# Making a product's operands one step later, and one low part by an accumulating DMA

## The chip, the cores and the metric

The kernel runs on one core of one Trainium2 chip. Its time is the device time of one execution in microseconds (us), given as the median of several runs; lower is better. The core has a matrix engine (TensorE, PE in the profile), a vector engine (VectorE, DVE), a scalar engine (ScalarE, ACT), GpSimd (POOL) and SyncE (SP), each with an instruction queue of its own that is worked through in order, and 16 DMA engines that SP, ACT and POOL can give transfers to. Engines wait for each other by semaphores.

## The reference

Two layers of a decoder trunk on 512 tokens of width 1024, in float32. What bears on the change is the feed-forward block (swiglu), of which there are two in each layer, so four in all:

```python
D_MODEL = 1024
SEQ = 512
DEPTH = 2
D_FF = 2816

def rms_norm(x, gain):
    xf = x.astype(jnp.float32)
    inv = lax.rsqrt(jnp.mean(xf * xf, axis=-1, keepdims=True) + NORM_EPS)
    return (xf * inv).astype(x.dtype) * gain

def swiglu(h, w_gate, w_up, w_down):
    return (jax.nn.silu(h @ w_gate) * (h @ w_up)) @ w_down

def reference(x, ...):
    for l in range(DEPTH):
        x = x + 0.5 * swiglu(rms_norm(x, ffn1_norm[l]), ffn1_wg[l], ffn1_wu[l], ffn1_wd[l])
        h = rms_norm(x, mix_norm[l])
        z = h @ w_in[l]
        ...
        x = x + jnp.concatenate([attn_out, conv_out], axis=-1) @ w_out[l]
        x = x + 0.5 * swiglu(rms_norm(x, ffn2_norm[l]), ffn2_wg[l], ffn2_wu[l], ffn2_wd[l])
    return rms_norm(x, final_norm)
```

## The kernel before

**Every float32 matrix is split in two.** TensorE multiplies fp32r tiles, a rounded form of float32. Each operand is made into a high part (a rounding cast on ScalarE) and a low part (the value less the high part, a subtraction on VectorE), by `split` (line 204); a product is then three matmuls: high by high, high by low, low by high. For the weights these parts are called `wh` and `wl` (pools of three buffers each), and line 205 and line 206 of the profile are the cast and the subtraction of every split in the kernel.

**Products of 2 x 2 blocks are made with seven multiplications instead of eight.** The class `Seven` (line 662) makes the seven operands of one side from four blocks b11, b12, b21, b22 of activations: b11, b21 and b22 as they are, and four sums t1 to t4 (lines 681 to 687: t1 = b11 - b12, which overwrites b12; t2 and t3 from b12 - b22; t4 = t2's value + b21). Each is then split into a pair of tiles named `fb...` or `ft...`, from a pool of eight. `make` makes an operand when it is first asked for. The seven operands of the other side are made from weights as `need_split` (line 215) goes along: its forms are a11, a12, s2, s3, s1, a22, s4 in the order of the seven products, two half tiles (h = 0, 1) each. The tiles are loaded by SP into a pool of eight raw buffers; the second summand of a weight sum is added by POOL in an accumulating DMA (line 200); s2 is made by an addition in place on VectorE (`tensor_add(a11, a11, s1)`, line 233) ahead of its split, and s4's input by another accumulating DMA (line 261).

**The shares.** In each feed-forward block two groups of 512 of the 2816 rows of `w_down` are worked off by `share` (line 895), so there are eight shares in the kernel: s_0_2 and s_0_6 in the first block, s_1_1 and s_1_5, s_2_1 and s_2_5, s_3_1 and s_3_5 in the others. A share goes through seven steps, one product each, written by `stream` (line 878) as 2 x 12 matmuls at line 884:

```python
CHAINS = (
    ("x", "b11", True), ("w", "b21", True), ("x", "t2", False), ("y", "t3", True),
    ("x", "t1", False), ("y", "t4", False), ("x", "b22", False),
)
```

The second name is the activations' operand and the first the accumulator (x_s, w_s, y_s in the profile). Step 2 is thus the product of t2 with the weights' sum s2. The first block's second share has its own order (`CHAINS_EARLY`: b11, b21, t3, t2, t4, t1, b22, the last into an accumulator of its own, z_s). After a step's last matmul VectorE adds the accumulator into the stream x (line 923).

Before the change, once step 0, 1 or 2 has been written, `share` asks for the operand of the step four on: after step 0 that of step 4, after step 1 that of step 5, after step 2 that of step 6. The operands of steps 0 to 3 have been made by then, during the stage ahead (`ahead`). The mixing stage calls `share` too, with a list of its own (`soon`), and makes its operands t1 and b22 by `split_far` (line 209), in which the low part is made without VectorE:

```python
    def split_far(hi, lo, raw):
        nc.scalar.activation(lo, raw, AF.Copy, scale=-1.0)
        state["cast"] = nc.scalar.copy(hi, raw)
        return nc.gpsimd.dma_start(out=f32(lo), in_=raw, accum_op=ALU.add)
```

ScalarE writes the negated rounded value into `lo` (line 211) and the rounded value into `hi` (line 212), and POOL issues a DMA (line 213) that adds the value itself into `lo`.

**The order of work.** Instructions are written in program order and a scheduler arranges each engine's queue from its own estimates and the buffers' dependences; some regions are arranged by hand (`by_hand`, from step 4 of the first block's second share on). So a call that is moved in the source moves instructions in the queues, and others close up around them.

Of the kernel before, what the change touches and what calls it, by code (L numbers as in the profile page):

```python
# [73 lines left out]
def trunk_kernel(  # L74
# [32 lines left out]
    def psum(tag, shape, name):  # L107
        return ps.tile(shape, F32, tag=tag, bufs={"mm": 4, "sc": 2, "aux": 2}[tag], name=name)
# [4 lines left out]
    def g8(name, dt=F32R, shape=(P, 2, 2, S)):  # L113
        return work.tile(list(shape), dt, tag="g8", bufs=4, name=name)
# [165 lines left out]
    def take_split(ahead=SPLIT_AHEAD):  # L280
        n = state["group"]
        state["group"] += 1
        need_split(n + ahead)
        return n, *split_of.pop(n)
# [20 lines left out]
    def by_hand():  # L305
        state["region"] = tc.manual_schedule(engines={pe})
        state["region"].__enter__()
# [180 lines left out]
    def xt(t, o):  # L488
        return stream_of[2 * o + t // 2][:, t % 2, :]
# [388 lines left out]
    def stream(accs, wh, wl, xh, xl, h, start, norm=None):  # L878

        for u in range(2):  # L880
            tok = slice(u * P, (u + 1) * P)
            for k in range(2):
                for i, (x_, w) in enumerate(((xh, wh), (xl, wh), (xh, wl))):
                    nc.tensor.matmul(  # L884
                        accs[u],
                        x_[:, 2 * h + k, tok],
                        w[:, k, :],
                        start=start and h + k + i == 0,
                        stop=h + k == 2 and i == 2,
                        skip_group_check=not start,  # L890
                    )
            if norm:
                norm.pull()

    def share(
        ops, by, between=None, soon=None, after=None, each=lambda: None, w=None, kept=()
    ):


        accs = {}  # L900
        chains, shares = (CHAINS_EARLY, SHARES_EARLY) if after else (CHAINS, SHARES)
        for step, (acc, operand, start) in enumerate(chains):
            ops.make(operand)
            if after and step == 4:
                by_hand()
            xh, xl = ops.forms[operand]
            if acc == "w" and w:
                accs[acc], start = w, False
            if start:
                tag = {"x": "mm", "y": "sc", "w": "aux", "z": "mm"}[acc]  # L910
                accs[acc] = [psum(tag, [P, S], f"{acc}_{ops.name}_{m}") for m in range(2)]
            for h in range(2):
                _, wh, wl = take_split()
                stream(accs[acc], wh, wl, xh, xl, h, start, after if step == 6 else None)
                each()
                if soon:
                    ops.make(*soon.get((step, h), ()))
                if h == 0 or step in kept:
                    continue
                for o, t, sign in shares[step]:  # L920
                    for m in range(2):
                        part = xt(2 * t + m, o)
                        nc.vector.scalar_tensor_tensor(  # L923
                            part, accs[acc][m], by * sign, part, op0=ALU.mult, op1=ALU.add
                        )
                        if after and (step, (o, t)) in ENDS_EARLY:
                            after(2 * t + m, o)
            if not soon and step < 3:
                ops.make(chains[step + 4][1])
            if between:  # L930
                between(step)
        return accs
# [5 lines left out]
    def ahead(ops, at):  # L938
        return lambda step: ops.make(*at.get(step, ()))


    def ffn(norm, stages, whole, after=None, late=None):
# [228 lines left out]
                pending.setdefault(clock[0] + tick, []).append(lambda do=do, n=n: do(n))  # L1171

        def shared(b):
            return Seven([raw_act(b), raw_act(b + 2)], room_form, f"s_{whole}_{b}")

        def raw_act(b):
            if b not in raws:
                raws[b] = g8(f"raw_a_{whole}_{b}", F32, (P, KC // 2, S))
            return raws[b]
# [13 lines left out]
        for i, (what, b) in enumerate(stages):  # L1193
# [3 lines left out]
            if what in "wu" and stages[i + 1][0] == "s":  # L1197
                ops = shared(sevens[0])
                if what == "w":
                    winograd2(b, i, ahead(ops, {3: ("b11",), 4: ("b21",), 5: ("t2",), 6: ("t3",)}))  # L1200
                else:
                    winograd(b, ahead(ops, {1: ("b11",), 2: ("b21",), 4: ("t2",), 6: ("t3",)}))
            elif what == "w":
                winograd2(b, i)
            if what == "s" and b == sevens[0]:
                then = shared(sevens[1])
                sums = ("t3", "t2") if stages[-1] == ("s", sevens[1]) else ("t2", "t3")
                soon = ahead(then, {3: ("b11",), 4: ("b21",), 5: sums[:1], 6: sums[1:]})
                goes_on = stages[i + 1][0] == "d"
                accs = share(ops, 0.5, soon, each=turns, kept=(1, 5, 6) if goes_on else (1,))  # L1210
                w = accs["w"]
                open_ = going_on(accs) if goes_on else {}
            elif what == "s":
                accs = share(
                    then,
                    0.5,
                    each=turns,
                    after=after if final else None,
                    w=w,
                    kept=() if final else (1, 5, 6),  # L1220
                )
                open_ = going_on(accs) if not final else {}
# [153 lines left out]
    def mix(l, norm, after):  # L1376
# [184 lines left out]
        ops.make("b21", "b22")  # L1561
        after.begin()
        share(ops, 1.0, soon={(0, 1): ("t3",), (1, 0): ("t2",), (1, 1): ("t1", "t4")}, after=after)
        state["late"] = None

# [42 lines left out]
```

## Time and profile before

| what | value |
|---|---|
| median of 3 runs | 1658.65 us (1658.05 to 1659.65) |
| the profiled execution, its own time | 1658.03 us |
| its span, first to last instruction | 1656.3 us |
| matmuls on PE | 7912 |
| mean granted TensorE clock | 0.999 |
| DMA moved | 299.77 MB, mean 181 GB/s |

The profile is one execution of the program, seen by the hardware's profiler. A row of a timeline gives the start from the span's beginning, the duration, the engine, the line of the kernel, the operation, the tiles written and read with buffer numbers left out, their shape, and how many such instructions follow each other; in brackets stands how long the engine had been idle before and what ended that. A row of waits gives who waited for whom, the total in us, how often, and the longest. A row of windows gives a stretch, its length, each engine's busy time with its number of instructions, then the granted clock, the share of the 16 DMA engines' time and GB/s. A row of DMA issues gives size and the median time from issue to landing. Matmuls are pipelined: a matmul's modelled end lies behind the start of the next one.

### The profile page before, as it was taken

How to read it: one execution, taken by the hardware profiler on the slowest of the kernel's cores; microseconds unless marked ns; L12 is line 12 of the kernel's file. 1: busy time of each engine (PE TensorE's matmuls, PEld its weight loads, DVE VectorE, ACT ScalarE, POOL GpSimd, SP SyncE). 2: the span in 40 equal slices, each digit the busy share in tenths (PEclk: the TensorE clock that was granted, in tenths of full speed). 3: DMA queues.
4: the chain of work that ended last, by engine and by line, in shares of the span. 5: the costliest groups of instructions: out<-in, count | busy, mean ns of one | idle time of the engine just before them, and what ended most of it. 6: DMA issues, size and time to landing. Idle time of an engine off the chain costs nothing.

```text
span 1656.3 us, 21592 instructions
## 1 busy us (share of the span) xinstructions
PE 1641.2 (99%) x7912; PEld 1377.6 (83%) x7912; DVE 1317.0 (80%) x1720; ACT 1084.7 (65%) x1519; POOL 182.3 (11%) x164
## 2 busy tenths in 40 slices
PE   9999999999999999999999999999999999999998
PEld 7888897888889888888898888888988888888886
DVE  7977779867799777789697777896587987777995
ACT  6457776556566567777465777865565765777864
POOL 0011111100111101111001111110001101111111
PEclk9999999999999999999999999999999999999999
DMA  9379998721395779999737789995125946899991
GB/s 255 91 189 209 230 217 235 202 78 52 105 242 125 193 188 218 214 228 238 207 84 197 192 215 222 240 229 171 52 64 146 222 116 167 217 223 221 247 240 58
DMA packets 269568, 299.77 MB, mean 181 GB/s; under 512 B 89205, under 2 KB 153749, under 8 KB 269461
## 3 DMA queue, kind: packets, MB, share of 16 engines
q1 hardware_dynamic: 231156, 223.27, 45.6%
q0 software_dynamic: 37600, 74.46, 26.5%
q8 instruction: 62, 1.02, 0.2%
q10 hardware_dynamic: 704, 0.66, 0.1%
q14 instruction: 46, 0.37, 0.1%
HBM read 263.74 MB, written 2.10 MB: 161 GB/s over the span
## 4 chain that ended last, share of the span: by engine, by line
PE 92%; DVE 6%; ACT 1%; issue 1%; DMA 0%; POOL 0%; DVEq 0%; ACTq 0%; POOLq 0%
PE x L884 25%; PE y L884 12%; PE x_s L884 10%; PE w L884 6%; PE y_s L884 5%; PE acc L296 4%; PE acc L297 4%; PE acc L299 4%; PE down L346 3%; PE acc L323 3%; PE w_s L884 2%; DVE wl L206 2%; PE x_m L884 2%; PE up L1009 1%; PE acc L782 1%; DVE x L923 1%
## 5 line engine op out<-in xcount | busy, mean ns | idle before, releaser
L205 ACT CAST wh<-raw 128x1024 fp32r<-128x1024 f32 (+1 forms) x493 | 514.6, 1045 | 414.8 <-PE y L884 62.0
L206 DVE TENSOR_TENSOR wl<-raw,wh 128x1024 fp32r<-128x1024 f32 (+1 forms) x493 | 596.5, 1213 | 222.6 <-ACT wh L205 214.4
L884 PE MATMUL x<-wh,fb 128*128 128x512 f32 x608 | 187.4, 389 | 0.1
L884 PE MATMUL x<-wh,ft 128*128 128x512 f32 x608 | 187.2, 389 | 0.0
L884 PE MATMUL y<-wh,ft 128*128 128x512 f32 x608 | 187.2, 389 | 0.0
L884 PEld LDWEIGHTS x<-wh,ft 128*128 128x128 f32 x608 | 114.1, 188 | 23.7
L884 PEld LDWEIGHTS y<-wh,ft 128*128 128x128 f32 x608 | 114.1, 188 | 23.7
L884 PEld LDWEIGHTS x<-wh,fb 128*128 128x128 f32 x608 | 113.9, 188 | 23.9 <-DVE x L1240 0.5
L884 PE MATMUL x<-wl,fb 128*128 128x512 f32 x304 | 118.3, 389 | 0.0
L884 PE MATMUL x<-wl,ft 128*128 128x512 f32 x304 | 118.3, 389 | 0.0
L884 PE MATMUL y<-wl,ft 128*128 128x512 f32 x304 | 118.3, 389 | 0.0
L1155 ACT COPY raw_a<-pt 128x1024 uint16<-128x1024 uint16 x76 | 103.4, 1360 | 4.9 <-DMA pt<-pl 4.9
L200 POOL DMA_DIRECT2D raw<-in_ffn_wu_dram x39 | 47.2, 1210 | 522.3 <-DMA raw<-in_ffn_wu_dram 329.0
L296 PE MATMUL acc<-hh,wh 128*128 128x512 f32 x240 | 94.6, 394 | 0.0
L299 PE MATMUL acc<-hh,wl 128*128 128x512 f32 x240 | 93.9, 391 | 0.0
L884 PE MATMUL w<-wh,fb 128*128 128x512 f32 x304 | 93.6, 389 | 0.0
L297 PE MATMUL acc<-hl,wh 128*128 128x512 f32 x240 | 93.6, 390 | 0.0
L884 PE MATMUL y_s<-wh,ft_s 128*128 128x512 f32 x256 | 79.2, 390 | 0.7 <-ACT wh L205 0.7
L884 PE MATMUL x_s<-wh,ft_s 128*128 128x512 f32 x256 | 78.3, 390 | 0.7 <-ACT wh L205 0.7
L200 POOL DMA_DIRECT2D raw<-in_ffn_wg_dram x39 | 47.1, 1217 | 275.7 <-DMA raw<-in_ffn_wu_dram 110.3
L884 PE MATMUL x_s<-wh,fb_s 128*128 128x512 f32 x240 | 73.9, 389 | 0.0
L233 DVE TENSOR_TENSOR raw<-raw,raw 128x1024 f32<-128x1024 f32 x58 | 70.4, 1219 | 0.5
(358 smaller groups left out, 3440.0 us busy)
## 6 DMA issues: line engine op xcount, KB each, us to landing
raw<-in_ffn_wu_dram SPq DMA_DIRECT2D x126, 512.0 KB, 4.9
raw<-in_ffn_wd_dram SPq DMA_DIRECT2D x104, 512.0 KB, 5.8
raw<-in_ffn_wg_dram SPq DMA_DIRECT2D x86, 512.0 KB, 4.7
raw<-in_ffn_wu_dram POOLq DMA_DIRECT2D x39, 512.0 KB, 7.5
raw<-in_ffn_wg_dram POOLq DMA_DIRECT2D x39, 512.0 KB, 5.9
raw<-in_w_in_dram SPq DMA_DIRECT2D x36, 512.0 KB, 3.9
raw<-in_ffn_wd_dram POOLq DMA_DIRECT2D x32, 512.0 KB, 7.0
raw<-raw POOLq DMA_DIRECT2D x20, 512.0 KB, 7.0
```

The lines of the kernel that those rows point to most:

```text
L200: nc.gpsimd.dma_start(out=r, in_=rows_of(*more), accum_op=ALU.add)
L205: cast = nc.scalar.copy(hi, raw)
L206: eng.tensor_sub(lo, raw, f32(hi))
L233: nc.vector.tensor_add(a11, a11, s1)
L296: nc.tensor.matmul(acc, hi[:, k, :], rhs[k][0], start=k == first, stop=False)
L297: nc.tensor.matmul(acc, hi[:, k, :], rhs[k][1], start=False, stop=False)
L299: nc.tensor.matmul(acc, lo[:, k, :], rhs[k][0], start=False, stop=k == last)
L323: nc.tensor.matmul(accs[j][:, t * H : (t + 1) * H], w[:, k, :], x_, start=t + k + i == 0, stop=k == KC - 1 and i == 2, skip_group_check=True,)
L346: nc.tensor.matmul(acc, a[:, k, tok], w[:, k, :], start=i + k + n == 0 and fresh[t], stop=i == last and k == 1 and n == 2, skip_group_chec ...
L782: nc.tensor.matmul(opening[n], (lo if part == "w" else hi)[:, k, :], xl if part == "x" else xh, start=n not in begun, stop=k == KC - 1 and ...
L884: nc.tensor.matmul(accs[u], x_[:, 2 * h + k, tok], w[:, k, :], start=start and h + k + i == 0, stop=h + k == 2 and i == 2, skip_group_chec ...
L1155: nc.scalar.copy(room.rearrange("p c (n z) -> p c z n", z=2)[:, :, z, :], turned[0][:, NT * z + 2 * c : NT * z + 2 * c + 2, :],)
```

## The change

```diff
@@ share
-            if not soon and step < 3:
-                ops.make(chains[step + 4][1])
+            if not soon:
+                ops.make(*[chains[n][1] for n in {1: (4,), 2: (6, 5)}.get(step, ())])
@@ ffn
         def shared(b):
-            return Seven([raw_act(b), raw_act(b + 2)], room_form, f"s_{whole}_{b}")
+            return Seven([raw_act(b), raw_act(b + 2)], room_form, f"s_{whole}_{b}", far=("b22",))
```

In the eight shares the operand of step 4 is asked for after step 1 instead of after step 0; after step 2 those of step 6 and of step 5 are asked for, in this order, where step 5's was asked for after step 1 before. The operand b22, of step 6, is split by `split_far` where it was split by `split`: for each share one subtraction on VectorE (line 206) is left out, one copy on ScalarE (line 211) is added, and one accumulating DMA of 512 KB from SBUF to SBUF on POOL's queue (line 213). The mixing stage and all other products are as before, and so are the numbers of matmuls and of loads.

## The prediction

> **What bounds the kernel now.** I read the page's busy times and chain first, then TensorE's waits, then the start times of its products where those waits lie, then VectorE's order just ahead of them.
>
> ```profile
> span 1656.3 us, 21592 instructions
> ...
> PE 1641.2 (99%) x7912; PEld 1377.6 (83%) x7912; DVE 1317.0 (80%) x1720; ACT 1084.7 (65%) x1519; POOL 182.3 (11%) x164
> ...
> PE 92%; DVE 6%; ACT 1%; issue 1%; DMA 0%; POOL 0%; DVEq 0%; ACTq 0%; POOLq 0%
> ```
>
> TensorE (PE) is busy in 99% of the span and carries 92% of the chain that ended last. The change leaves the number of products alone, so it can only give or take time in which TensorE waits. The view of waits, for TensorE, has these rows among seven (who waited, for whom: total us, times, longest):
>
> ```profile
> PE acc L323 <- DVE wl L206: 1.9, 3, 0.6
> PE x_s L884 <- DVE wl L206: 1.1, 1, 1.1
> PE y_s L884 <- ACT wh L205: 0.7, 3, 0.2
> PE x_s L884 <- ACT wh L205: 0.7, 1, 0.7
> ```
>
> x_s, y_s and w_s are the sums of the eight groups that the change touches (called shares here: two in each of the four feed-forward blocks). They wait 1.1 + 0.7 + 0.7 = 2.5 us. The acc row lies in other stages and stays. But 2.5 is not the price: a matmul's modelled end reaches past the start of the next, so the first part of a delay shows no idle time. The price is read from starts. These are the timeline's first matmuls of a product (a step, 24 matmuls): step 1 writes w_s, step 4 is the first x_s after the y_s of step 3.
>
> ```profile
> 738.55 0.39 PE L884 MATMUL w_s<-wh,fb_s 128*128 128x512 f32 x1
> 754.87 0.39 PE L884 MATMUL x_s<-wh,ft_s 128*128 128x512 f32 x1
> 776.63 0.39 PE L884 MATMUL w_s<-wh,fb_s 128*128 128x512 f32 x1
> 793.49 0.39 PE L884 MATMUL x_s<-wh,ft_s 128*128 128x512 f32 x1
> 255.68 0.39 PE L884 MATMUL w_s<-wh,fb_s 128*128 128x512 f32 x1
> 268.86 0.39 PE L884 MATMUL y_s<-wh,ft_s 128*128 128x512 f32 x1
> ```
>
> The first two rows, a share without a wait: 754.87 - 738.55 = 16.32 us for three steps, so 5.44 us a step, 0.227 a matmul. The second share of the same block: 793.49 - 776.63 = 16.86, so 0.54 lost. The very first share: 268.86 - 255.68 = 13.18 for two steps (10.88), so 2.30 lost. Where it is lost, by the timeline:
>
> ```profile
> 261.93 1.20 PE L884 MATMUL x_s<-wh,ft_s 128*128 128x512 f32 x4 [0.65 <-ACT wh L205]
> 264.18 0.50 PE L884 MATMUL x_s<-wl,ft_s 128*128 128x512 f32 x1 [1.05 <-DVE wl L206]
> 783.39 0.73 PE L884 MATMUL y_s<-wh,ft_s 128*128 128x512 f32 x2 [0.25 <-ACT wh L205]
> ```
>
> All of it stands in step 2, and each time TensorE waits for that step's weights, never for an operand. The y_s row of waits has three entries of at most 0.2 (0.7 in total): one in the second share of each of the last three blocks, 0.54 each. Waiting in all shares: 2.30 + 3 x 0.54 = 3.92 us.
>
> **What makes those weights late.** Step 2's weights are sums; L233 adds two loaded tiles in place on VectorE, after which ScalarE casts (wh) and VectorE subtracts (wl). VectorE in the second share, before:
>
> ```profile
> 773.13 1.22 DVE L206 TENSOR_TENSOR wl<-raw,wh 128x1024 fp32r<-128x1024 f32 x1
> 774.27 1.22 DVE L685 TENSOR_TENSOR raw_a<-raw_a 128x1024 f32<-128x1024 f32 x1
> 775.41 1.22 DVE L206 TENSOR_TENSOR wl<-raw,wh 128x1024 fp32r<-128x1024 f32 x1
> 776.54 1.28 DVE L923 SCALAR_TENSOR_TENSOR x<-x_s,x 128x512 f32<-128x512 f32 x2
> 777.74 1.21 DVE L206 TENSOR_TENSOR ft_s<-raw_a,ft_s 128x1024 fp32r<-128x1024 f32 x1
> 778.87 2.35 DVE L233 TENSOR_TENSOR raw<-raw,raw 128x1024 f32<-128x1024 f32 x2
> 781.14 1.21 DVE L687 TENSOR_TENSOR sums_s<-sums_s,raw_a 128x1024 f32<-128x1024 f32 x1
> 782.28 1.21 DVE L206 TENSOR_TENSOR wl<-raw,wh 128x1024 fp32r<-128x1024 f32 x1
> ```
>
> L685 and the ft_s behind it make t1, which is not used until step 4; L687 belongs to t4, for step 5. These three stand ahead of step 2's wl. The operation pitch is 1.14 us (773.13, 774.27, 775.41).
>
> **The change part by part.** *Later making.* The built program's order after the change puts the first addition where L685 stood (774.27), then wl (775.41), the two updates of x (776.54), the second addition (777.74), step 2's first wl (778.88), L685 (780.02), the second wl (781.15), L687, t1's low part, step 3's first wl (784.57). TensorE needs the first wl at its third matmul: 776.63 + 5.44 + 2 x 0.227 = 782.52. It is done at 780.1, 2.4 early, where it was done at 783.49. The second, done at 782.4, is needed 2.72 later than the first, at 785.24; step 3's, done at 785.8, at 787.96. So the 0.54 goes, three times: **-1.62**. In the first share before:
>
> ```profile
> 258.37 1.22 DVE L206 TENSOR_TENSOR ft_s<-raw_a,ft_s 128x1024 fp32r<-128x1024 f32 x1
> 259.50 2.35 DVE L233 TENSOR_TENSOR raw<-raw,raw 128x1024 f32<-128x1024 f32 x2
> 261.78 1.22 DVE L687 TENSOR_TENSOR sums_s<-sums_s,raw_a 128x1024 f32<-128x1024 f32 x1
> 262.91 2.39 DVE L206 TENSOR_TENSOR wl<-raw,wh 128x1024 fp32r<-128x1024 f32 x2
> ```
>
> After, the first addition has moved to before 258.37, and the slots from there are: wl, second addition, L685, L687, and at 262.91 the second wl, done at 264.13. Step 2 would start unhindered at 255.68 + 5.44 = 261.12; the first wl is done by 259.6, and the second is needed at 261.12 + 2.72 + 0.45 = 264.29. That is 0.16 of room, so I count 0.1 as left over (0 to 1.2, one operation late). **-2.2** of the 2.30. The addition that moves forward there, some 8 us, finds its second summand: that load's DMA stands on POOL at
>
> ```profile
> 232.36 1.19 POOL L200 DMA_DIRECT2D raw<-in_ffn_wd_dram  x1 [12.48 <-DVE wl L206]
> ```
>
> which is 18 us ahead of the new place.
>
> *What is now later.* t1 (t4 in the first block's second share, whose products stand in another order) is called two steps ahead of its use, the sixth operand also two, the seventh three: 10.9, 10.9 and 16.3 us, against some 4 us of additions, cast and subtraction. t4's low part follows the x updates that close step 2, about 790.5, and is needed at 776.63 + 4 x 5.44 = 798.4. If that cover went, each operation late would cost 1.14. Cost 0, bounds 0 to 1.
>
> *The seventh's low part.* Per share one subtraction of 1.2 us leaves VectorE, one copy (L211) joins ScalarE, busy 65%, and one DMA joins POOL's queue, busy 11%. The mixing stage does the same on the same shape:
>
> ```profile
> L211 ACT ACTIVATE fb_m<-m x2: 1057/1057/1057, 466.2 to 1283.8; 128x1024 fp32r<-128x1024 f32 x2
> fb_m<-m POOLq DMA_DIRECT2D x2, 512.0 KB, 6.6
> 745.87 1.05 ACT L205 CAST ft_s<-sums_s 128x1024 fp32r<-128x1024 f32 x1
> 765.75 0.39 PE L884 MATMUL x_s<-wh,fb_s 128*128 128x512 f32 x1
> ```
>
> L211 takes the slot at 745.87 in the block's first share; the DMA goes out about 747 and lands 6.6 later, near 754. Step 6 reads it from 765.75: 11 us of room. On ScalarE step 3's second weight cast stands behind L211, 1 us later with 2.7 us of a half step in hand. On POOL the DMA waits for L211 alone, and behind it stand the accumulating loads of the next share's sums, which go out at 764.77 and were waiting for SP's loads; SP's own order is unchanged. Cost 0, if these loads land in time:
>
> ```profile
> 764.77 2.49 POOL L200 DMA_DIRECT2D raw<-in_ffn_wd_dram  x2 [24.59 <-DMA raw<-in_ffn_wd_dram]
> raw<-in_ffn_wd_dram POOLq DMA_DIRECT2D x1, 512.0 KB, 8.1
> raw<-in_ffn_wd_dram POOLq DMA_DIRECT2D x1, 512.0 KB, 10.0
> 745.00:758.00 13.00, 13.00 (x59) 10.78 (x58) 12.88 (x14) 9.21 (x11) 0.00 (x0) 1.00 0.99 225
> 758.00:770.00 12.00, 12.00 (x54) 9.94 (x54) 11.97 (x13) 9.57 (x10) 2.42 (x3) 1.00 1.04 329
> q0 software_dynamic: 37600, 74.46, 26.5%
> ```
>
> The last but one number of a window's row is the DMA share: 0.99 and 1.04, all 16 engines full just where the new DMA falls. POOL's queue q0 holds 26.5% of 1656.3 us in 142 transfers (74.46 MB by 0.524): 3.1 us of all engines each. So what follows can land up to 3.1 later. The two loads land at 764.77 + 8.1 = 772.9 and about 766.0 + 10.0 = 776.0; the moved additions want them at 774.27 and 777.74. With a delay d, the second addition starts at 776.0 + d, and step 3's first wl, 8.0 after it, is done at 784.0 + d against 787.96: free up to d = 3.9. I take 0 (bounds 0 for d up to 3.1, and the price below).
>
> [...]
>
> **Sum.** -1.62 - 2.2 = -3.8 us. The profiled execution took 1658.03 (span 1656.3, 1.7 around it), so 1654.2 by itself; the median of the three runs is 1658.65, 0.6 above it, so **1654.8** against that.
>
> **Rivals.**
> - *The first share stays late.* Its room is 0.16 us, and one operation or a late cast takes it: 1.1 and the restart, about 1.2 back: 1656.0. The pitch of 1.14 holding speaks against it.
> - *The wait moves.* Full DMA engines bring d to between 4 and 5, and VectorE, which works in order, stands at the moved additions with the next wl behind them. At d = 5.2 the three later blocks lose 1.3 each and all is given back: 1658.6. For it: shares of 0.99 and 1.04. Against it: d is 3.1 at most by the packets.
> - *Slower, by the same place.* If the new DMA displaces loads for its whole landing time, d = 6.6, additions start 2.7 past what is free, three times: 8.1 lost, 3.8 gained, 1663.0. It is slower than before from d = 5.2, by 0.2% from 6.3.
> - *It does not do what it says.* The built order shows the subtraction gone and the additions ahead; only an in-order engine held up earlier could undo it: 1658.6.
>
> **How the numbers follow.** 0.2% (3.3 us, 1655.3) is about what a measurement can tell from no change. Forecast 0.62, its own range 1653.2 to 1655.8, of which 0.06 lies within 0.2%; first share late 0.14; wait moves 0.10; nothing done 0.02; slower 0.12. So faster 0.56, same 0.06 + 0.14 + 0.10 + 0.02 = 0.32, slower 0.12. The range runs from 1653.2 to 1658.6: it takes in the two middle cases and leaves out the slower one and the tails.
>
> **What would show it.** Right: no wait of x_s or y_s in TensorE's waits; 16.3 us from step 1 to step 4 in every share; the acc row still 1.9; fb_s low parts landing over 5 us ahead of step 6. Wrong: VectorE idle before L233 on a DMA (the wait moved), TensorE waiting for fb_s on a DMA, or step 2 of the first share still over 5.6 us.

## The result and the profile after

The changed kernel takes 1656.3 us (median of 12 runs, 1653.37 to 1657.61), the kernel before beside it 1658.96 us (12 runs, 1658.05 to 1662.69). The ratio, taken over paired runs, is 0.9978 with a 95% interval of 0.9970 to 0.9985: between 2.5 and 5.0 us faster. The profiled execution took 1655.61 us, 2.42 less than that of before.

The page of the changed kernel:

```profile
span 1653.8 us, 21619 instructions
...
PE 1639.9 (99%) x7912; PEld 1377.6 (83%) x7912; DVE 1307.0 (79%) x1712; ACT 1092.4 (66%) x1527; POOL 192.7 (12%) x172
...
q0 software_dynamic: 41824, 78.65, 28.1%
```

Eight instructions have left VectorE and eight have joined ScalarE and POOL, as the change says. The eight new DMAs raised queue q0's share of the DMA engines from 26.5% to 28.1% of the span.

TensorE's waits in the changed kernel, all six rows (total us, times, longest):

```profile
PE acc L323 <- DVE wl L206: 1.9, 3, 0.6
PE x_m L884 <- DVE wl L206: 1.6, 2, 0.8
PE idle L141 <- DVE warm L728: 1.2, 1, 1.2
PE down L346 <- DVE x L1240: 0.9, 2, 0.5
PE up L1009 <- DVE wl L206: 0.8, 3, 0.3
PE xt L747 <- DMA x<-in_x_dram: 0.3, 1, 0.3
```

No x_s, y_s or w_s is left. The down and xt rows are new. They lie in the first 120 us, ahead of all that the change touches.

The starts of steps in the changed kernel, from TensorE's timeline (two steps of the first share, then step 1 and step 4 of the other three blocks' second shares):

```profile
256.85 0.39 PE L884 MATMUL w_s<-wh,fb_s 128*128 128x512 f32 x1
267.76 0.61 PE L884 MATMUL y_s<-wh,ft_s 128*128 128x512 f32 x2
775.52 0.39 PE L884 MATMUL w_s<-wh,fb_s 128*128 128x512 f32 x1
792.21 0.39 PE L884 MATMUL x_s<-wh,ft_s 128*128 128x512 f32 x1
1102.18 0.39 PE L884 MATMUL w_s<-wh,fb_s 128*128 128x512 f32 x1
1118.50 0.39 PE L884 MATMUL x_s<-wh,ft_s 128*128 128x512 f32 x1
1592.35 0.62 PE L884 MATMUL w_s<-wh,fb_s 128*128 128x512 f32 x2
1608.67 0.62 PE L884 MATMUL x_s<-wh,ft_s 128*128 128x512 f32 x2
```

The first share's two steps now take 10.91 us (13.18 before, 10.88 without a wait). The second shares take 16.69, 16.32 and 16.32 (16.86 before, 16.32 without a wait). So 3.92 us of waiting have become 0.03 + 0.37 = 0.40: 3.52 us gained inside the shares.

Of these, 1.1 us do not show in the two profiles' spans. The kernel before began its first share at 250.21, the changed one at 251.38, 1.17 later. From there to the last matmul it is 1398.99 us before and 1395.40 after, a gain of 3.59. Two more profiles of the changed kernel (below) began the share at 250.65 and 250.80, and other kernels of this study between 249.83 and 252.74. The start of the program varies by itself, and the change has no part in it.

What did get worse is seen in two rows of the cost groups that the chain of waits does not show. Of before and, in the second fence, of after:

```profile
L1155 ACT COPY raw_a<-pt 128x1024 uint16<-128x1024 uint16 x76 | 103.4, 1360 | 4.9 <-DMA pt<-pl 4.9
```

```profile
L1155 ACT COPY raw_a<-pt 128x1024 uint16<-128x1024 uint16 x76 | 103.3, 1359 | 13.0 <-DMA pt<-pl 12.9
...
L233 DVE TENSOR_TENSOR raw<-raw,raw 128x1024 f32<-128x1024 f32 x58 | 70.8, 1221 | 2.3 <-DMA raw<-in_ffn_wd_dram 1.6
```

L1155 is the copy by which ScalarE brings the activations of one stage into the raw tiles of another: SP turns each of four tiles with a DMA transpose (pt from pl), then `join` copies the result. ScalarE stood 13.0 us ahead of these copies where it had stood 4.9; 8.7 of the 13.0 lie in the three blocks whose second shares follow, where it had not stood at all before. VectorE stood 1.6 us ahead of the additions for a load. Neither cost much, as the next views show. VectorE in the second block's second share, after:

```profile
775.53 1.22 DVE L233 TENSOR_TENSOR raw<-raw,raw 128x1024 f32<-128x1024 f32 x1 [0.96 <-DMA raw<-in_ffn_wd_dram]
...
779.00 1.22 DVE L233 TENSOR_TENSOR raw<-raw,raw 128x1024 f32<-128x1024 f32 x1
780.13 1.22 DVE L206 TENSOR_TENSOR wl<-raw,wh 128x1024 fp32r<-128x1024 f32 x1
781.27 1.22 DVE L685 TENSOR_TENSOR raw_a<-raw_a 128x1024 f32<-128x1024 f32 x1
...
785.81 1.22 DVE L206 TENSOR_TENSOR wl<-raw,wh 128x1024 fp32r<-128x1024 f32 x1
```

The order is the one forecast: addition, wl, x, addition, wl, L685. The share begins 1.11 us earlier than before (775.52 against 776.63), so the forecast start of the second addition, 777.74, stands at 776.63 here; it ran at 779.00, 2.4 late. Step 2's first wl is done at 780.13 + 1.22 = 781.35 and was wanted at the third matmul of 780.96, at 781.41. Step 3's (785.81) is done at 787.03, wanted at 786.97. That is how the 0.37 is lost. POOL, in the same stage:

```profile
746.11 1.30 POOL L213 DMA_DIRECT2D fb_s<-raw_a  x1 [6.59 <-ACT fb_s L211]
766.79 1.19 POOL L200 DMA_DIRECT2D raw<-in_ffn_wd_dram  x1 [19.39 <-DVE wl L206]
768.15 1.21 POOL L200 DMA_DIRECT2D raw<-in_ffn_wd_dram  x1 [0.16 <-issue]
```

The new DMA went out at 746.11. It landed 8.5 us later, at 754.6, 10 us ahead of step 6, which reads it from 764.64. The two loads of the sums, forecast at 764.77 - 1.11 = 763.66 if nothing held them, went out at 766.79, 3.1 late. The row names a subtraction of VectorE as what POOL waited for, but POOL was past its wait at 766.23 (each of these loads goes out some 0.55 us behind that), and the subtraction ended at 765.28 + 1.22 = 766.50. What POOL waits for are the tiles to which its loads add, and SP loads these. The landing of the first is not in the trace; those for POOL's next three loads land at 767.57, 771.63 and 774.11, and POOL gets past its waits at 767.59, 771.66 and 774.14. SP's queue shows why they are late, before and, in the second fence, after:

```profile
749.13 6.30 SPq L1103 DMA_TRANSPOSE pt<-pl  x4
755.53 0.52 SPq L189 DMA_DIRECT2D raw<-in_ffn_wd_dram  x1
```

```profile
748.34 9.05 SPq L1103 DMA_TRANSPOSE pt<-pl  x4
757.51 1.68 SPq L189 DMA_DIRECT2D raw<-in_ffn_wd_dram  x1
```

SP issues the four transposes and, right behind them, the loads. Beside the new DMA the transposes held SP for 9.05 us instead of 6.30 (10.13 instead of 7.21 and 9.44 instead of 6.21 in the other two blocks). Against its share, the first load behind them went out 3.1 us later than before, which is the whole delay of POOL's loads. The late transposes hold ScalarE too:

```profile
760.71 1.35 ACT L1155 COPY raw_a<-pt 128x1024 uint16<-128x1024 uint16 x1 [3.20 <-DMA pt<-pl]
```

So two chains begin at the new DMA, both by way of the transposes. One goes through SP's queue: transposes late, SP's loads behind them late, POOL's loads late, additions late. The other goes through ScalarE's: transposes late, L1155 late, a weight's cast and subtraction behind it late. In this share the first ends last: VectorE was ready for the addition at 774.57 and stood 0.96 us for the load, which landed at 775.43. The prediction had DMA to loads, without the transposes. The experiments ask which half of the change brought the gain, and which of the two chains counts where.

### The profile page after: what moved, and what is told of

It is laid out like the page before. It is cut to its first block, busy times and chain, and to the rows that moved or that the text cites. A ratio compares the mean times of both kernels' runs of the same rounds, so it can differ in the third digit from the quotient of the medians.

```text
span 1653.8 us, 21619 instructions
## 1 busy us (share of the span) xinstructions
PE 1639.9 (99%) x7912; PEld 1377.6 (83%) x7912; DVE 1307.0 (79%) x1712; ACT 1092.4 (66%) x1527; POOL 192.7 (12%) x172
## 3 DMA queue, kind: packets, MB, share of 16 engines
q0 software_dynamic: 41824, 78.65, 28.1%
## 4 chain that ended last, share of the span: by engine, by line
PE 92%; DVE 5%; ACT 1%; issue 1%; DMA 0%; POOL 0%; DVEq 0%; ACTq 0%; POOLq 0%
PE x L884 25%; PE y L884 12%; PE x_s L884 10%; PE w L884 6%; PE y_s L884 5%; PE acc L296 4%; PE acc L297 4%; PE acc L299 4%; PE down L346 3%; PE w_s L884 3%; PE acc L323 3%; PE x_m L884 2%; DVE wl L206 2%; PE up L1009 1%; PE acc L782 1%; DVE x L923 1%
## 5 line engine op out<-in xcount | busy, mean ns | idle before, releaser
L1155 ACT COPY raw_a<-pt 128x1024 uint16<-128x1024 uint16 x76 | 103.3, 1359 | 13.0 <-DMA pt<-pl 12.9
L233 DVE TENSOR_TENSOR raw<-raw,raw 128x1024 f32<-128x1024 f32 x58 | 70.8, 1221 | 2.3 <-DMA raw<-in_ffn_wd_dram 1.6
```

Of the source, the lines that this page charges most:

```text
L233: nc.vector.tensor_add(a11, a11, s1)
L1155: nc.scalar.copy(room.rearrange("p c (n z) -> p c z n", z=2)[:, :, z, :], turned[0][:, NT * z + 2 * c : NT * z + 2 * c + 2, :],)
```

## The experiments

**Theory:** the gain is that of the later making alone; the DMA is hidden where the additions have been moved forward, and costs by ScalarE's chain where they have not. **Rivals:** the subtraction taken off VectorE is what counts; or the DMA costs nothing at all; or it delays the sums' loads, without ScalarE. Every kernel ran beside the kernel before on the same chip; on the three chips used this took 1659.91, 1660.47 and 1659.82 us (26, 27 and 27 runs), and each ratio is against the one of its own chip.

**Only the later making.** The changed kernel without its second edit:

```diff
-            return Seven([...], room_form, f"s_{whole}_{b}", far=("b22",))
+            return Seven([...], room_form, f"s_{whole}_{b}")
```

> The later making alone: the operands are made at the changed kernel's places, the seventh's low part by VectorE's subtraction as before, no new DMA. Theory (the gain is the later making; the new DMA only takes some of it back by delaying loads): no wait of x_s or y_s, 16.3 us from step 1 to step 4 in every share, VectorE not idle before L233 on a DMA, time about 3.9 us under the kernel before, 1655.0, some 1 us faster than the changed kernel. Rival (the gain comes from the subtraction taken off VectorE): waits of x_s and y_s still some 2.5 us in all, time within 1 us of the kernel before.

Measured: 1655.67 us (11 runs), ratio 0.9976 (0.9968 to 0.9985). From the first share's start to the last matmul it is 1395.32 us, against 1395.40 with both edits; it is not the 1 us faster than the changed kernel that was expected. ScalarE stands 6.7 us ahead of L1155 in place of 13.0, SP is held by the transposes for 6.52 us in the second block in place of 9.05, and all second shares take 16.32. The whole gain is here without the DMA, which falsifies the rival that the subtraction counts.

**Only the DMA.** The kernel before with the second edit:

```diff
-            return Seven([...], room_form, f"s_{whole}_{b}")
+            return Seven([...], room_form, f"s_{whole}_{b}", far=("b22",))
```

> The accumulating DMA alone: the operands are asked for at the places of the kernel before, b22's low part by ScalarE's copy and POOL's DMA. Theory: the additions of L233 stay behind the making of t1, so the 2.30 us of the first share and 0.54 in each of the three later blocks stay; loads land some 3 us later, which nothing feels because the additions are late anyway: 1658.5 to 1660. Rival (VectorE's relief makes the gain): 1656 to 1657.

Measured: 1664.17 us (10 runs), ratio 1.0025 (1.0016 to 1.0034): 2.7 to 5.6 us slower. The expectation missed; the DMA alone costs more than a few tenths. TensorE's waits in it:

```profile
PE x_s L884 <- DVE wl L206: 2.9, 4, 1.2
...
PE x_s L884 <- ACT wh L205: 1.1, 1, 1.1
```

The last block's second share shows ScalarE's chain, on ScalarE, VectorE and TensorE in three timelines of this kernel:

```profile
1581.01 1.35 ACT L1155 COPY raw_a<-pt 128x1024 uint16<-128x1024 uint16 x1 [3.30 <-DMA pt<-pl]
```

```profile
1583.31 1.23 DVE L206 TENSOR_TENSOR wl<-raw,wh 128x1024 fp32r<-128x1024 f32 x1 [2.99 <-ACT wh L205]
...
1599.39 2.35 DVE L233 TENSOR_TENSOR raw<-raw,raw 128x1024 f32<-128x1024 f32 x2
```

```profile
1591.46 0.50 PE L884 MATMUL x_s<-wl,fb_s 128*128 128x512 f32 x1 [0.45 <-DVE wl L206]
...
1604.07 0.50 PE L884 MATMUL x_s<-wl,ft_s 128*128 128x512 f32 x1 [1.20 <-DVE wl L206]
```

ScalarE stands 3.30 for the transposes, VectorE 2.99 for the cast behind that copy, and the additions run when TensorE already wants their sums. VectorE does not stand for a load ahead of them here: in this order they come so late that the loads have landed. By the starts of the steps, step 6 and the next share's step 0 take 11.74 us instead of 10.88, and the three steps behind them 17.86 instead of 16.32: 0.9 and 1.5 lost. The sum of ScalarE's waits ahead of L1155 is smaller here (9.1) than in the changed kernel (13.0), which is faster: what counts is the room behind the wait, and the additions have none here.

All shares of this profile together lose 4.5 + 0 + 0.5 + 2.4 = 7.4 us, 3.5 more than the 3.92 of before, which is also the difference from the first share to the last matmul (1402.43 against 1398.99). In the second block's second share, where the kernel before loses 0.54, this one loses nothing. The first share's 4.5 are not of the chain: its two stalls are the ones of before, 1.07 and 1.06 in place of 0.65 and 1.05, and the rest is a drop of the clock to 0.50 for 3.41 us, told in the last section. The profiled execution (1661.40) is one of the fastest of its ten runs (1660.52 to 1667.09); what makes the median 2.8 us slower is not seen in a trace.

**No DMA in the first shares of the blocks.** The changed kernel, with `far` in the second shares only:

```diff
-            return Seven([...], room_form, f"s_{whole}_{b}", far=("b22",))
+            return Seven([...], room_form, f"s_{whole}_{b}", far=("b22",) if b != sevens[0] else ())
```

> The changed kernel, but the accumulating DMA only in the second share of each block; the first share's b22 is split on VectorE. Theory (only the first share's DMA delays the loads that the additions wait for): VectorE not idle on a DMA before L233, 16.3 us from step 1 to step 4 everywhere, 1655.0, as with the later making alone. Rival (any of the DMAs delays something): 1656.3, as the changed kernel.

Measured: 1655.65 us (9 runs), ratio 0.9975 (0.9965 to 0.9984); 5.1 us of L1155 waits, no loss in any share, 1395.13 us from the first share to the end. It is the first share's DMA that meets the transposes: without it they hold SP for 6.0 to 6.3 us in the three blocks. Its removal is worth 0.3 us in the trace; in the runs it can't be told from the change.

**Two operands by DMA.** The second shares' b11 as well; in the second block its DMA goes out at 751.95, between the first of the transposes (750.04) and the second (752.97):

```diff
-            return Seven([...], room_form, f"s_{whole}_{b}", far=("b22",))
+            return Seven([...], room_form, f"s_{whole}_{b}", far=("b22", "b11") if b != sevens[0] else ("b22",))
```

> The changed kernel with one more accumulating DMA in the same stretch: the second share's b11, made during the first share, is split the same way. Theory (each such DMA holds all DMA engines some 3.1 us, and the loads land by so much later): the accumulating loads before L233 land 6 to 7 us later than in the kernel before, past the 3.9 us that are free; VectorE idles there, TensorE waits 2 to 5 us in each of the three later blocks: 1663 to 1672. Rival (the DMA is hidden, VectorE's relief counts): 1655 to 1656.5.

Measured: 1669.97 us (6 runs), ratio 1.0060 (1.0045 to 1.0074). With twice the suspected cause in the same place both chains grow: ScalarE stands 24.7 us ahead of L1155 in place of 13.0, VectorE 10.2 us ahead of the additions in place of 2.3, and TensorE loses 10.7 us in its waits for x_s and w_s, which the changed kernel doesn't have. (The profiled execution, 1674.06 us, is the slowest of the six.) The cover that hides one DMA does not hide two.

**The copies later, with the DMA alone.** If the DMA cost by ScalarE standing at L1155, then the same late transposes should cost little once L1155 stands further back. In the three blocks concerned `join` is moved by two half steps (5.4 us), in the kernel with the DMA alone:

```diff
-            plan += [(6 + 2 * gap + gap * n, join, n) for n in range(4)]
+            plan += [((8 if stages[at + 1][0] == "s" else 6) + 2 * gap + gap * n, join, n) for n in range(4)]
```

> The accumulating DMA alone (operands asked for as in the kernel before), and ScalarE's four copies of the turned activations (L1155) asked for two half steps later in the three later blocks. Theory (the new DMA delays the DMA transposes, and ScalarE, working in order, waits for them at L1155 with the next weights' casts behind it, so VectorE stands idle some 3 us and its additions come late): VectorE's idle time of 2 to 3 us behind L1155 is gone, the second shares fall back to 0.54 us lost each, time 1 to 3 us under the accumulating DMA alone, 1661 to 1663. Rival (the loads that the additions wait for land late, L1155 does not matter): as the accumulating DMA alone, 1664.

Measured: 1659.42 us (11 runs), ratio 0.9993 (0.9984 to 1.0002), where the DMA alone had 1.0025 (1.0016 to 1.0034) on another chip: less time than either side expected. In its profile, the slowest of its runs (1663.25 us), the last block's second share lost nothing, but the second block's 0.5 us and the third's 1.2, where VectorE stood 0.89 and 1.35 for a load ahead of an addition: SP's chain, from the DMA to the sums' loads, is there too. So both kernels were run again, on one chip.

> The DMA alone again, now on the same chip as the kernel with the later copies, for their two times came from two chips. Both theories: 1662 to 1666 us, ratio 1.001 to 1.0035, ScalarE waiting 7 to 11 us ahead of L1155.

> The DMA alone with the copies L1155 two half steps later. If most of the DMA's cost goes by way of ScalarE's copies: 3 us or more under the DMA alone on the same chip (1658 to 1661). If the loads of the sums are delayed directly and the earlier difference was the chips': within 1.5 us of the DMA alone, with VectorE waiting for a load ahead of L233 in most second shares.

Measured: the DMA alone 1665.90 us (5 runs), ratio 1.0037 (1.0024 to 1.0050), a little above what was expected; with the later copies 1659.42 us (11 runs), ratio 0.9995 (0.9986 to 1.0004). That is 6.5 us between them by the medians. The third block shows the cause. First the transposes' landing times there (tile pt, 1070 to 1105) in the kernel before, then the same line of the two kernels with ScalarE's and TensorE's rows:

```profile
DMA to landing us min/median/max: 4.4/4.7/5.0
```

With the DMA alone:

```profile
DMA to landing us min/median/max: 5.2/7.8/10.3
```

```profile
1091.04 1.36 ACT L1155 COPY raw_a<-pt 128x1024 uint16<-128x1024 uint16 x1 [3.31 <-DMA pt<-pl]
```

```profile
1106.62 0.39 PE L884 MATMUL w_s<-wh,fb_s 128*128 128x512 f32 x1
1124.43 0.39 PE L884 MATMUL x_s<-wh,ft_s 128*128 128x512 f32 x1
```

With the DMA alone and the copies later:

```profile
DMA to landing us min/median/max: 6.8/7.5/8.2
```

```profile
1089.85 1.35 ACT L1155 COPY raw_a<-pt 128x1024 uint16<-128x1024 uint16 x1
```

```profile
1102.51 0.39 PE L884 MATMUL w_s<-wh,fb_s 128*128 128x512 f32 x1
1118.83 0.39 PE L884 MATMUL x_s<-wh,ft_s 128*128 128x512 f32 x1
```

The transposes are as late in the second as in the first, but ScalarE waits for none of them, and steps 1 to 3 take 16.32 us instead of 17.81. In this profile all three second shares take 16.32. The DMA's traffic is the same, only the place where ScalarE meets it has moved. This is the run that shows the chain by ScalarE in the kernel with the DMA alone. How large it is, it shows less well. Each profile is of the fastest of its runs; 3.2 us of their difference lie in the three blocks, 1.5 in the first share, which the edit does not touch. And 16.32 is less than the 16.86 of the kernel before, so the later copies also took away what these shares lose without the DMA; the copies later without the DMA were not run.

**The copies later, with the whole change.** The same edit on the changed kernel:

> The changed kernel with L1155 two half steps later in the three later blocks. Theory: the waits for the DMA transposes fall from 13 to under 6 us, VectorE is not idle before step 6's first wl of the first share, every second share takes 16.3 us from step 1 to step 4; time as the later making alone, 1655.7, not separable from the changed kernel by more than 1 us. Rival: 0.3 to 0.4 us still lost in a second share, VectorE idle before L233 on a DMA.

Measured: 1655.66 us (5 runs), ratio 0.9966 (0.9954 to 0.9979), the lowest of the study, with 5.6 us of L1155 waits. But of the three second shares, all expected at 16.3, the last block's takes 16.77, and VectorE stands 6.5 us ahead of the additions, as the rival had it. The changed kernel beside it:

> The changed kernel once more, beside the three others on one chip, to read its shares in a second execution. Theory: from the first share's start to the last matmul 3.5 to 3.9 us less than in the kernel before; of its second shares one or none loses up to 0.4 us, and the time is within 1 us of 1656.3. Rival (the loss in the second shares grows where loads land later): over 1 us lost in them, 1657.5 or more.

Measured: 1656.07 us (11 runs), ratio 0.9976 (0.9967 to 0.9985); from the first share's start to the last matmul it is 2.87 us less than before, under the 3.5 to 3.9 expected. The two were then run once more, on another chip:

> The whole change with the copies later. If the chain by ScalarE costs the changed kernel what the traces show (0.4 to 1.1 us): 1655 to 1656, 0.4 to 1 under the changed kernel. Rival: the same as the changed kernel within 0.3.

> The changed kernel on the same chip, for comparison: 1655.8 to 1656.6, ratio 0.997 to 0.9985.

Measured: 1656.53 us (11 runs), ratio 0.9978 (0.9969 to 0.9987) with the later copies, and 1656.33 us (11 runs), ratio 0.9981 (0.9972 to 0.9990) without. The advantage did not come back: later copies take L1155's waits from 14.1 to 3.7 us and the time stays. The profile shows where the wait went, on VectorE and POOL in the second block's second share, with the copies later:

```profile
775.83 1.23 DVE L233 TENSOR_TENSOR raw<-raw,raw 128x1024 f32<-128x1024 f32 x1 [3.47 <-DMA raw<-in_ffn_wd_dram]
```

```profile
766.83 1.19 POOL L200 DMA_DIRECT2D raw<-in_ffn_wd_dram  x1 [19.64 <-DVE ft_s L206]
```

ScalarE does not stand at L1155 here, and POOL's load still goes out only 3.0 us ahead of the share's first matmul (3.3 in the changed kernel, 6.4 before): the transposes hold SP for 11.54 us. VectorE now stands 3.47 us for the load where it stood 0.96, this share loses 0.9 us and the third block's 0.7. So in the second block of the changed kernel it is SP's chain that sets what is lost, and later copies leave it as it is. This rests on the traces: no run put SP's loads ahead of the transposes.

The two new profiles of the changed kernel show how thin that room is. In the first of them the first share loses 0.5 us and the second block's second share 0.6. In the other the first share loses 1.6 and the third block's second share 0.6. The 1.6 begin ahead of the first new DMA (which goes out near 268), with a load that lands late, on ScalarE's timeline:

```profile
252.53 1.05 ACT L205 CAST wh<-raw 128x1024 fp32r<-128x1024 f32 x1 [2.58 <-DMA raw<-in_ffn_wd_dram]
```

The profiles of three other kernels with the DMA have the same late load there, ScalarE standing 2.2 to 2.8 us for it, also ahead of their first new DMA. Why it is late in some executions was not followed.

**The DMA one step later.** Step 6's operand asked for after step 3, to move the DMA behind the transposes:

```diff
-                ops.make(*[chains[n][1] for n in {1: (4,), 2: (6, 5)}.get(step, ())])
+                ops.make(*[chains[n][1] for n in {1: (4,), 2: (5,), 3: (6,)}.get(step, ())])
```

> The changed kernel with the seventh operand asked for after step 3 instead of 2, so that its DMA is issued some 5 us later, behind the DMA transposes. Theory (what the new DMA delays first are the transposes): ScalarE's wait at L1155 is back near the 5 us of the kernel before, no second share loses time: 1655.7. Rival (it is the loads): the DMA falls on the loads that the additions wait for, which land at least as late as in the changed kernel, and the second shares lose 0.4 us or more each: 1656.5 to 1658.

Measured: 1660.53 us (11 runs), ratio 0.9998 (0.9989 to 1.0007), outside what either side expected. TensorE in the last block's first share, step 6, then ScalarE shortly before it:

```profile
1586.83 0.50 PE L884 MATMUL x_s<-wl,fb_s 128*128 128x512 f32 x1 [0.53 <-DVE wl L206]
```

```profile
1583.26 1.35 ACT L1155 COPY raw_a<-pt 128x1024 uint16<-128x1024 uint16 x1 [5.18 <-DMA pt<-pl]
```

In this block the DMA went out at 1568.58, 0.1 us ahead of the first transpose (1568.68) and not behind the four. Those landed 8.3 us after issue in the median (5.6 in the changed kernel's same stretch), and ScalarE stood 5.18 where it had stood 2.7; now step 6's own weights are late, which no moved addition could cover. A loss of 1.8 us in the first share, of the kind just told of, is in this profile too, so not all that it loses is the DMA's.

## Why the prediction was right, and where its steps were not

- **The bound.** Right: only TensorE's waiting could be won, and it was won by starts, not by the 2.5 us of shown idle time (0.40 us of 3.92 are left).
- **Where the time was lost.** Right as to the cause, but one row was misread. The y_s row at 783.39 is not step 2's: y_s is step 3's sum, and two of its products stand ahead of step 2's first low part in the built order. TensorE waited there for the last of three casts that come close together, behind the additions:

```profile
780.20 3.14 ACT L205 CAST wh<-raw 128x1024 fp32r<-128x1024 f32 x3 [3.09 <-DVE raw L233]
```

  The additions are the late party by either reading, and the sum does not change.
- **Later making, three second shares, -1.62.** Measured -0.17 - 0.54 - 0.54 = -1.25. The order on VectorE came as forecast, and the experiment without the DMA gave the whole 1.62, so the 0.37 is put down to the DMA.
- **The first share, -2.2.** Measured -2.27 (13.18 to 10.91), -1.8 and -0.7 in three profiles. The room of 0.16 us was as thin as it was called, and the rival that the first share stays late comes true in some executions.
- **What is now later, cost 0.** No wait of TensorE for t1, t4 or the sixth operand is seen.
- **The new DMA, cost 0.** It cost 0.37 us in the profiled execution. The step named the right party, the sums' loads, and the delay at their issue, 3.1 us, equals its estimate from the packets; that the size came out is luck as far as is shown, for the way was another. The step counted the DMA engines' work and POOL's queue, and took SP's part as settled because "SP's own order is unchanged". It left out that SP's DMA transposes stand in that queue ahead of the loads: beside the new DMA they hold SP 2.75 us longer. It also left out ScalarE's copies, which wait for the transposes with weights behind them. And the 3.9 us that it called free held for the second load alone. The second addition follows the first by 3.47 us on VectorE (775.53 to 779.00), so a second addition at 776.0 + 3.9 = 779.9 means a first one at 776.4, which leaves its load, at 772.9, only 3.5; against its share it landed 3.7 later than before. Where the additions had not been moved, the DMA costs 2.7 to 5.6 us, and 4.0 to 8.3 in the repetition; in the traces what the blocks lose comes by way of ScalarE, for the room of the moved additions is missing. The landing, 6.6 by the mixing stage's row, was 8.5 in the second block and 8.0 in the median of the eight.
- **The sign for "wrong".** VectorE idle before L233 on a DMA was put down as the mark of a moved wait. It came, 0.96 us in the second block and 0.66 in the third, and yet 0.37 us was lost in the one and nothing in the other. A wait on an engine off the path is a mark only once its room is known.
- **The sum.** -3.8 forecast; -3.52 inside the shares and -3.59 from the first share to the end; by the runs -2.5 to -5.0. The medians differ by 2.7 only. In the profiled pair the remainder is the start (1.17 us); for the medians this is not shown.
- **The rivals.** The slower case (d = 6.6, additions 2.7 past what is free) did not come. What it described, additions too late for TensorE, is what the DMA does in the kernel before, by way of ScalarE, and with two operands, where VectorE stands 10.2 us ahead of the additions. "The wait moves" came in part: the wait did move to the moved additions, but at a delay of 3 to 4 us and not 5, so most of the gain stayed.

## What to carry to other kernels

When work is moved from a full engine to a DMA, list every transfer that is in flight in that window and every queue that waits for one of them in order, those that issue further transfers too, and not only the queue that the DMA is put on; here the DMA went on POOL's queue, and the late parties stood in SP's and ScalarE's. Test the parts of a change alone: one of these two edits gave all of the gain, and the other costs 2.7 us or more without the first. And when a copy waits in an in-order queue for a transfer that other traffic can delay, moving the copy back by the room that it has can take the delay off the path, as it did with the DMA alone; but first see which wait ends last, for in the changed kernel the same edit only moved the wait from ScalarE to VectorE.

## What was not expected of the hardware

**Stalls of about 2 us in all were followed by half the clock for 3.41 us, in some executions.** In the kernel with the DMA alone TensorE stalls twice in the first share, 1.07 and 1.06 us. The view of windows (length, busy time of each engine with its instructions, then granted clock, DMA share and GB/s) for the 3.41 us of the drop and the 3.41 ahead of it:

```profile
261.28:264.69 3.41, 1.35 (x5) 0.67 (x4) 3.41 (x5) 3.28 (x4) 1.76 (x2) 1.00 0.62 116
264.69:268.10 3.41, 3.35 (x8) 2.70 (x9) 3.41 (x4) 3.08 (x3) 0.00 (x0) 0.50 1.09 202
```

TensorE is idle for 2.06 us of the first stretch and gets half the clock for the whole of the second. Eight matmuls start in it, 0.425 us apart (265.35, 266.20 and 267.05 for each second one) instead of 0.227: about 1.6 us lost, beside the stalls. The kernel with two operands by DMA has such a drop from 785.12 to 788.53, behind a single stall of 2.03 us, and another from 1102.56 to 1105.97, both at a granted clock of 0.50. The kernel before stalls in the same place for 0.65 and 1.05 us, and its clock stays:

```profile
259.52:262.93 3.41, 2.76 (x12) 1.80 (x10) 3.41 (x5) 2.10 (x2) 1.42 (x2) 1.00 0.79 146
262.93:266.34 3.41, 2.36 (x10) 1.80 (x10) 3.41 (x4) 3.41 (x5) 0.35 (x1) 1.00 1.03 196
```

These two stretches part the stalls. One laid over both, 260.90 to 264.31, holds 1.71 us of idle time, and its clock and that of the next 3.41 us are 1.00. In the second profile of the kernel with the DMA alone the same two stalls are 1.08 and 1.04 us long and end 2.25 us apart (264.55 and 266.80; 2.24 in the first, at 262.51 and 264.75), and the matmuls behind them go on 0.23 us apart, without a drop.

The four drops that the views show came behind 2.06 us of idle time (DMA alone), 2.03 and 1.68 (two operands by DMA, the 1.68 in a stretch of 3.50) and 1.85 (DMA alone with the copies later, ahead of 266.97), each in the 3.4 to 3.5 us ahead of the drop. The 1.71 above were not followed by one, nor were the 1.08 and 1.04, together 2.12 us in the 3.41 up to 266.80, and neither was a single stall of 1.20 us (at 1604.07 above). So the idle time alone does not part these executions, and what decides is not shown. Two stalls near a microsecond cost 1.6 us more in one execution of the kernel with the DMA alone and nothing more in the other. Whether this is why its times spread over 6.6 us (10 runs), and those of the kernel before beside it over 4.6 (26 runs), no run shows.
